# First loads into the third stage buffer, more loads ahead of the first store, and two loads issued as unequal pieces

## The chip, the cores and the metric

The kernel runs on one core of a Trainium2 chip (trn2); the other cores are idle. The metric is device time in microseconds, median of the fast runs. A profile is one execution; its span leaves out some 2 us of the time. PE is the matrix engine, DVE the vector engine, ACT the scalar engine and SP the engine that issues most transfers; HBM is the large memory, SBUF the memory beside the engines, PSUM the small one that PE writes. Transfers run on sixteen DMA engines; "the queue" is what has been issued and has not landed.

## The reference, cut to what matters

```python
batch, seq, heads, dim = 16, 512, 16, 64            # all float32
q1, q2 = q[..., :32], q[..., 32:]
q_rot = concat([q1 * cos - q2 * sin, q1 * sin + q2 * cos])   # k_rot likewise
scores = einsum('bshd,bthd->bsht', q_rot, k_rot)    # 16 x 512 x 16 x 512
```

Inputs are 67 MB, the output is 268 MB. Every byte crosses between HBM and SBUF once.

## The kernel before

It has 64 stages: four for each of the 16 batches. A stage makes 4 MB of scores: DVE rotates k and q rows ("rope", three operations each), PE transposes them into a PSUM "bank", DVE or ACT copies the bank to kT_t or qT_t, PE multiplies, ACT copies scores to the stage buffer `st` (three buffers of 32 KB per partition), and SP issues the store. Loads come in pairs of row blocks, 1 MB each. Batch 0 is cut by heads instead, so that stores of 1 MB can start early. Its eight loads have runs of G x D = 256 elements, 1 KB:

```python
    def load_unit(which, u):                # batch 0: 8 loads of 512 KB
        t = in_tiles.get((which, u // 2))
        if t is None:
            t = in_tile(which, u // 2)      # takes an input buffer: k has 3, q has 2
        src = (k_v if which == "k" else q_v)[0, :, :, G * u : G * (u + 1), :]
        nc.sync.dma_start(t[:, u % 2].rearrange(...), src)
    def load_pair(which, pair):             # later batches: one load of 1 MB
        ...
        nc.sync.dma_start(t.rearrange("p c (h d) -> p c h d", h=H), src)
    ...
        for i in range(C):                  # stages 0 to 3, C = 4
            ...
            for p in range(HP):             # 8 score pairs of a stage
                scores(i, p, st)
                if p in (1, 2) and late:    # k rows of batch 1
                    bank, dst = transposed(*late.pop(0))
                    dve.pop(0)()
                    nc.vector.tensor_copy(out=dst, in_=bank)
                if p == 5:
                    ...
                    tr_act(...)             # transposes that ACT copies
                if p == 7:
                    ...
        for i in range(C, NST):             # stages 4 to 63
            ...
            if i % 2 == 1:
                load_pair("q", (i + 1) // 2 + 2)
            else:
                load_pair("k", (i + 4) // 2 + 3)
            ...
            for p in range(HP):
                scores(i, p, st)            # the store is issued with the last pair
```

## Time and profile before

| | kernel before |
|---|---|
| time | 814.07 us, median of 3 runs (811.2 to 814.53) |
| span of the profiled run | 810.0 us |
| transfers | 336.31 MB, 415 GB/s over the span, 432 by the usual time of a 32 KB packet |
| busiest compute engine | PE, 83% of the span |
| first 4 MB store issued | 79.90 us |
| last store: median of its sixteen parts, last part | 798.8, 808.9 us |

The prediction shows the lines that carry this. A store is done by sixteen DMA engines, each of which reports its own landing; the last row of the table is read from those events in the trace. Where below I give the mean idle time of the DMA engines, it is counted from the packets in the trace: the time in which an engine has no packet, averaged over sixteen.

### The profile page before, as it was taken

How to read it: one execution, taken by the hardware profiler on the slowest of the kernel's cores; microseconds unless marked ns; L12 is line 12 of the kernel's file. 1: busy time of each engine (PE TensorE's matmuls, PEld its weight loads, DVE VectorE, ACT ScalarE, POOL GpSimd, SP SyncE). 2: the span in 40 equal slices, each digit the busy share in tenths (PEclk: the TensorE clock that was granted, in tenths of full speed). 3: DMA queues.
4: the chain of work that ended last, by engine and by line, in shares of the span. 5: the costliest groups of instructions: out<-in, count | busy, mean ns of one | idle time of the engine just before them, and what ended most of it. 6: DMA issues, size and time to landing. Idle time of an engine off the chain costs nothing.

```text
span 810.0 us, 7781 instructions
## 1 busy us (share of the span) xinstructions
PE 676.1 (83%) x3072; PEld 297.1 (37%) x3072; DVE 598.7 (74%) x624; ACT 500.1 (62%) x533; POOL 0.7 (0%) x6
## 2 busy tenths in 40 slices
PE   4997999888887888978888888888888889889960
PEld 2443444333333333333333333333333334334310
DVE  7798988877777877868868688677778787786300
ACT  3884777656565675566666656665656657566770
POOL 0000000000000000000000000000000000000000
PEclk9998999999999999999999999999999999999995
DMA  8999999999999999999999999999999999999994
GB/s 272 383 424 397 426 428 426 433 418 431 434 424 432 433 422 434 433 421 438 431 420 437 432 420 438 432 420 438 432 417 442 409 421 440 428 386 435 398 417 202
DMA packets 29028, 336.31 MB, mean 415 GB/s; under 512 B 3392, under 2 KB 7744, under 8 KB 15424
## 3 DMA queue, kind: packets, MB, share of 16 engines
q1 hardware_dynamic: 27648, 335.55, 98.1%
q8 instruction: 24, 0.39, 0.2%
q10 hardware_dynamic: 1344, 0.26, 0.2%
q14 instruction: 12, 0.10, 0.0%
HBM read 67.37 MB, written 268.44 MB: 415 GB/s over the span
## 4 chain that ended last, share of the span: by engine, by line
DMA 58%; PE 22%; DVE 8%; ACT 8%; issue 1%; ACTq 0%
DMA out_dram<-st 57%; PE ps L159 16%; ACT st L166 8%; PE bank L136 6%; DVE part L118 3%; DVE k_rot L121 2%; DVE k_rot L115 1%; DVE q_rot L121 1%; DVE q_rot L115 1%; DVE qT_t L259 1%; DMA sin_k<-in_sin_dram 1%; DVE kT_t L215 0%; ACT kT_t L176 0%; ACTq L286 0%; ACTq L166 0%
## 5 line engine op out<-in xcount | busy, mean ns | idle before, releaser
L166 ACT COPY st<-ps 128x1024 f32<-128x1024 f32 x512 | 488.9, 1022 | 275.0 <-DMA out_dram<-st 176.4
L159 PE MATMUL ps<-kT_t,qT_t 64*128 64x512 f32 x2048 | 528.0, 637 | 72.1 <-ACT st L166 69.4
L159 PEld LDWEIGHTS ps<-kT_t,qT_t 64*128 64x128 f32 x2048 | 183.6, 194 | 255.3 <-issue 148.3
L259 DVE COPY qT_t<-bank 128x512 f32<-128x512 f32 x118 | 81.6, 691 | 135.7 <-PE bank L136 135.1
L136 PE MATMUL bank<-ident,k_rot 128*128 128x128 f32 x512 | 84.6, 291 | 35.7 <-DVE k_rot L121 35.6
L136 PEld LDWEIGHTS bank<-ident,k_rot 128*128 128x128 f32 x512 | 55.1, 143 | 132.7 <-DVE k_rot L121 69.0
L136 PEld LDWEIGHTS bank<-ident,q_rot 128*128 128x128 f32 x512 | 58.4, 149 | 99.8 <-issue 74.8
L259 DVE COPY kT_t<-bank 128x512 f32<-128x512 f32 x112 | 77.0, 688 | 24.2 <-PE bank L136 24.2
L136 PE MATMUL bank<-ident,q_rot 128*128 128x128 f32 x512 | 90.0, 304 | 1.9 <-DVE q_rot L121 1.9
L121 DVE TENSOR_TENSOR k_rot<-k_rot,part 128x1024 f32<-128x1024 f32 x64 | 78.4, 1224 | 2.1
L115 DVE TENSOR_TENSOR q_rot<-q_sb,cos_q 128x1024 f32<-128x1024 f32 x64 | 78.0, 1219 | 0.0
L121 DVE TENSOR_TENSOR q_rot<-q_rot,part 128x1024 f32<-128x1024 f32 x64 | 77.8, 1216 | 0.2
L118 DVE TENSOR_TENSOR part<-q_sb,ss_q 128x1024 f32<-128x1024 f32 x64 | 77.8, 1216 | 0.0
L115 DVE TENSOR_TENSOR k_rot<-k_sb,cos_k 128x1024 f32<-128x1024 f32 x64 | 77.8, 1216 | 0.0
L118 DVE TENSOR_TENSOR part<-k_sb,ss_k 128x1024 f32<-128x1024 f32 x64 | 77.8, 1216 | 0.0
L176 ACT COPY kT_t<-bank 128x512 f32<-128x512 f32 x10 | 5.6, 619 | 6.6 <-PE bank L136 6.6
L215 DVE COPY kT_t<-bank 128x512 f32<-128x512 f32 x6 | 4.1, 685 | 4.5 <-PE bank L136 4.5
L176 ACT COPY qT_t<-bank 128x512 f32<-128x512 f32 x10 | 5.6, 618 | 2.6 <-PE bank L136 2.6
L59 DVE COPY ss_k<-sin_k 128x128 f32<-128x128 f32 x1 | 0.2, 227 | 5.3 <-DMA sin_k<-in_sin_dram 5.3
L176 ACT ACT_TABLE_LOAD x1 | 1.3, 1283 | 2.9 <-issue 2.9
masks.py:199 POOL TENSOR_SCALAR_AFFINE_SELECT ident<-ident 128x128 f32<-128x128 f32 x1 | 0.3, 292 | 0.1
L60 DVE TENSOR_SCALAR ss_q<-sin_q 128x128 f32<-128x128 f32 x1 | 0.2, 222 | 0.0
(7 smaller groups left out, 1.0 us busy)
## 6 DMA issues: line engine op xcount, KB each, us to landing
out_dram<-st SPq DMA_DIRECT2D x60, 4096.0 KB, 28.1
k_sb<-in_k_dram SPq DMA_DIRECT2D x30, 1024.0 KB, 19.1
q_sb<-in_q_dram SPq DMA_DIRECT2D x30, 1024.0 KB, 27.2
out_dram<-st SPq DMA_DIRECT2D x16, 1024.0 KB, 9.9
k_sb<-in_k_dram SPq DMA_DIRECT2D x4, 512.0 KB, 7.0
q_sb<-in_q_dram SPq DMA_DIRECT2D x4, 512.0 KB, 8.4
cos_k<-in_cos_dram ACTq DMA_DIRECT2D x1, 64.0 KB, 4.2
sin_k<-in_sin_dram ACTq DMA_DIRECT2D x1, 64.0 KB, 4.1
```

The costliest lines, as they stand in the source:

```text
L59: nc.vector.tensor_copy(out=ss[:, :, 0, :], in_=tabs["sin", which])
L60: nc.vector.tensor_scalar_mul(ss[:, :, 1, :], tabs["sin", which], -1.0)
L115: lambda: nc.vector.tensor_tensor(a.rearrange(v1, **k1), src.rearrange(v1, **k1), cs, op=mult),
L118: lambda: nc.vector.tensor_tensor(bt.rearrange(v1, **k2), src.rearrange(v1, **k2), ss, op=mult),
L121: lambda: nc.vector.tensor_tensor(a4, a4, swapped, op=add),
L136: nc.tensor.transpose(bank[:, x, :], src, ident)
L159: nc.tensor.matmul(out=ps[:, r, :], lhsT=lhs[64 * r : 64 * r + 64, :], rhs=rhs[64 * r : 64 * r + 64, :], start=True, stop=True,)
L166: nc.scalar.copy(out=st[:, 2 * p : 2 * p + 2, :], in_=ps)
L176: nc.scalar.copy(out=dst, in_=bank)
L215: nc.vector.tensor_copy(out=dst, in_=bank)
L259: nc.vector.tensor_copy(out=dst, in_=bank)
```

## The change

It has four parts. Batch 0 goes into the third stage buffer, in four loads, of which the larger two have 3 KB runs. That leaves the input buffers free, so that seven megabytes instead of five are asked for before the first store and two more loads come between the first stores. In stages 0 to 3 the transposes move to earlier score pairs and the tables are built on ACT; after that the load of a stage moves behind its store. Last, k pairs 16 and 20 are issued as nine pieces of unequal size.

```diff
-        nc.vector.tensor_copy(out=ss[:, :, 0, :], in_=tabs["sin", which])
-        nc.vector.tensor_scalar_mul(ss[:, :, 1, :], tabs["sin", which], -1.0)
+        nc.scalar.copy(out=ss[:, :, 0, :], in_=tabs["sin", which])
+        nc.scalar.mul(ss[:, :, 1, :], tabs["sin", which], -1.0)
...
+    PIECES = {
+        ("k", 16): (15, 14, 12, 10, 8, 7, 4, 10, 48),
+        ("k", 20): (15, 13, 11, 9, 6, 5, 3, 2, 64),
+    }
...
+    st_first = [stage_pool.tile([P, H, S], fp32, tag="stage", name="st") for _ in range(2)]
+    early = stage_pool.tile([P, 2 * C * H * D], fp32, tag="stage", name="early")
...
-        nc.sync.dma_start(t.rearrange("p c (h d) -> p c h d", h=H), src)
+        t = t.rearrange("p c (h d) -> p c h d", h=H)
+        p0 = 0
+        for n in PIECES.get((which, pair), (P,)):
+            nc.sync.dma_start(t[p0 : p0 + n], src[p0 : p0 + n])
+            p0 += n
...
-        for u in range(2):
-            load_unit("k", u)
-            load_unit("q", u)
-        for which in ("k", "q"):
-            for u in range(2, C):
-                load_unit(which, u)
+        for head, heads in ((0, G), (G, H - G)):
+            load_units("k", head, heads)
+            load_units("q", head, heads)
         load_pair("k", 2)
+        load_pair("q", 2)
+        load_pair("k", 3)
...
-                if p in (1, 2) and late:
+                if p in (0, 1) and late:
...
+                if i == 0 and p == 1:
+                    load_pair("k", 4)
+                if i == 0 and p == 3:
+                    load_pair("q", 3)
+                if p in (2, 6):
...
-            if i % 2 == 1:                      # stages 4 to 63: ahead of the score pairs
-                load_pair("q", (i + 1) // 2 + 2)
-            else:
-                load_pair("k", (i + 4) // 2 + 3)
...
+            if i % 2 == 1:                      # now behind the store
+                load_pair("q", (i + 1) // 2 + 2)
+            else:
+                load_pair("k", (i + 4) // 2 + 3)
```

More of the change, by code (lines that the diff above doesn't have):

```diff
@@ L71, in in_tile, with load_units @@
         return t
-    def load_unit(which, u):
-        t = in_tiles.get((which, u // 2))
-        if t is None:
-            t = in_tile(which, u // 2)
-        src = (k_v if which == "k" else q_v)[0, :, :, G * u : G * (u + 1), :]
-        nc.sync.dma_start(t[:, u % 2].rearrange("p (c h d) -> p c h d", c=C, h=G), src)
+    st_first = [stage_pool.tile([P, H, S], fp32, tag="stage", name="st") for _ in range(2)]
+    early = stage_pool.tile([P, 2 * C * H * D], fp32, tag="stage", name="early")
+    units = {}
+    def load_units(which, head, heads):
+        n = C * heads * D
+        t = early[:, load_units.used : load_units.used + n]
+        load_units.used += n
+        t = t.rearrange("p (c e) -> p c e", c=C)
+        src = (k_v if which == "k" else q_v)[0, :, :, head : head + heads, :]
+        nc.sync.dma_start(t.rearrange("p c (h d) -> p c h d", d=D), src)
+        for h in range(0, heads, G):
+            units[which, (head + h) // G] = t[:, :, D * h : D * (h + G)]
+    load_units.used = 0
     def load_pair(which, pair):
@@ L87, in load_pair @@
         src = (k_v if which == "k" else q_v)[b, :, 2 * x : 2 * x + 2]
-        nc.sync.dma_start(t.rearrange("p c (h d) -> p c h d", h=H), src)
+        t = t.rearrange("p c (h d) -> p c h d", h=H)
[3 more added lines that the diff above has]
+            p0 += n
     rots = {}
     def rope(which, n):
-        src = in_tiles[which, n // 2][:, n % 2]
         a = rot_pool.tile([P, H * D], fp32, tag="rot_" + which, name=which + "_rot")
@@ L99, in rope @@
         if n < C:
+            src = units[which, n]
+            sv = "p c (g j) -> p c g j"
             v1 = "p (c g j) -> p c g j"
@@ L105, in rope @@
         else:
+            src = in_tiles[which, n // 2][:, n % 2]
+            sv = "p (g j) -> p g j"
             v1 = "p (g j) -> p g j"
@@ L115, in rope @@
             lambda: nc.vector.tensor_tensor(
-                a.rearrange(v1, **k1), src.rearrange(v1, **k1), cs, op=mult
+                a.rearrange(v1, **k1), src.rearrange(sv, j=HD), cs, op=mult
             ),
             lambda: nc.vector.tensor_tensor(
-                bt.rearrange(v1, **k2), src.rearrange(v1, **k2), ss, op=mult
+                bt.rearrange(v1, **k2), src.rearrange(sv, j=D), ss, op=mult
             ),
@@ L184 @@
         load_tables("q", "(p c) j -> p c j")
-        for u in range(2):
-            load_unit("k", u)
-            load_unit("q", u)
-        for which in ("k", "q"):
-            for u in range(2, C):
-                load_unit(which, u)
+        for head, heads in ((0, G), (G, H - G)):
+            load_units("k", head, heads)
+            load_units("q", head, heads)
         load_pair("k", 2)
+        load_pair("q", 2)
+        load_pair("k", 3)
         make_identity(nc, ident)
         build_table("k")
+        build_table("q")
         run(rope("k", 0))
         tr_act("k", 0)
-        build_table("q")
         run(rope("q", 0))
@@ L201 @@
         for i in range(C):
-            st = stage_pool.tile([P, H, S], fp32, tag="stage", name="st")
+            st = st_first[i] if i < 2 else stage_pool.tile([P, H, S], fp32, tag="stage", name="st")
             late = []
@@ L207 @@
                 dve = rope("k", i + 1) + rope("q", i + 1) + rope("k", C + i)
+                nxt = [("k", i + 1), ("q", i + 1)]
             else:
                 dve = rope("q", C) + rope("k", C + i) + rope("q", C + 1) + rope("k", 2 * C)
+                nxt = [("q", C), ("k", C + i)]
             for p in range(HP):
                 scores(i, p, st)
-                if p in (1, 2) and late:
+                if p in (0, 1) and late:
                     bank, dst = transposed(*late.pop(0))
@@ L215 @@
                     nc.vector.tensor_copy(out=dst, in_=bank)
-                if p == 5:
-                    run(dve[: 3 if i == 0 else 1])
-                    dve = dve[3 if i == 0 else 1 :]
-                    tr_act(*(("k", i + 1) if i < C - 1 else ("q", C)))
-                if p == 7:
-                    run(dve[:3])
-                    dve = dve[3:]
-                    tr_act(*(("q", i + 1) if i < C - 1 else ("k", C + i)))
-            run(dve)
-            if i == 0:
-                load_pair("k", 3)
-                load_pair("q", 2)
-            elif i == 2:
-                load_pair("k", 4)
-                load_pair("q", 3)
+                if i == 0 and p == 1:
[3 more added lines that the diff above has]
+                if p in (2, 6):
+                    m = len(dve) - (6 if p == 2 else 3) + (-3 if i == C - 1 else 0)
+                    run(dve[:m])
+                    dve = dve[m:]
+                    tr_act(*nxt.pop(0))
+            run(dve)
+            if i == 1:
                 load_pair("k", 5)
```

## The prediction

> **What bounds the kernel now.** I read the page of the kernel before from the top: busy shares, slices, then the groups of instructions, then the chain that ended last, and last the table of windows for the first 80 us and the last 30 us.
>
> ```profile
> PE 676.1 (83%) x3072; PEld 297.1 (37%) x3072; DVE 598.7 (74%) x624; ACT 500.1 (62%) x533; POOL 0.7 (0%) x6
> DMA  8999999999999999999999999999999999999994
> GB/s 272 383 424 397 426 428 426 433 418 431 434 424 432 433 422 434 433 421 438 431 420 437 432 420 438 432 420 438 432 417 442 409 421 440 428 386 435 398 417 202
> DMA packets 29028, 336.31 MB, mean 415 GB/s; under 512 B 3392, under 2 KB 7744, under 8 KB 15424
> ...
> out_dram<-st SPq DMA_DIRECT2D x60, 4096.0 KB, 28.1
> ```
>
> No compute engine is full; the transfers are: tenths of 9 in every slice but the first and last, about 430 GB/s in the middle. A slice is 20.25 us. 336.31 MB at 430 GB/s would take 782 us, so of the span of 810.0 us some 28 us are lost, and the low numbers say where: 272, 383 and 397 in the first four slices, 386 and 398 near the end, 202 in the last. A 4 MB store lands 28.1 us after its issue though it moves in 9.7 us, so the queue is normally some 18 us deep: short waits of the compute engines cost nothing in the middle. In the chain of waits 57% is stores landing; before 140 us it is instead a run of DVE and PE pieces.
>
> The windows of the start (columns: stretch, length, busy time and count of PE, PEld, DVE, ACT, POOL, then granted clock, DMA share, GB/s):
>
> ```profile
> 6.00:8.00 2.00, 0.00 (x0) 0.00 (x0) 1.97 (x3) 0.00 (x0) 0.00 (x0) 1.00 1.10 357
> 16.00:18.00 2.00, 2.00 (x8) 0.93 (x6) 2.00 (x3) 0.84 (x1) 0.00 (x0) 1.00 0.93 369
> 18.00:20.00 2.00, 2.00 (x10) 0.86 (x10) 1.97 (x3) 1.62 (x3) 0.00 (x0) 1.00 0.03 10
> 20.00:22.00 2.00, 2.00 (x11) 0.70 (x8) 2.00 (x3) 2.00 (x3) 0.00 (x0) 1.00 0.79 328
> ```
>
> While the first batch comes in 1 KB runs the rate is about 350. At 18 us the five megabytes asked for are in and the first store is issued only at 19.59 us: the transfers stand still for about 2.5 us. The same view at the end:
>
> ```profile
> 796.00:798.00 2.00, 0.00 (x0) 0.00 (x0) 0.00 (x0) 0.00 (x0) 0.00 (x0) 0.50 1.18 508
> 798.00:800.00 2.00, 0.00 (x0) 0.00 (x0) 0.00 (x0) 0.00 (x0) 0.00 (x0) 0.50 0.16 66
> 802.00:804.00 2.00, 0.00 (x0) 0.00 (x0) 0.00 (x0) 0.00 (x0) 0.00 (x0) 0.50 0.11 49
> ```
>
> From 798 us on only one to three of sixteen engines still move bytes. The trace's sixteen landing times of the last store say it exactly: thirteen parts at 798.8 to 798.9 us, the others at 800.7, 804.4 and 808.9. The slowest DMA engine alone makes the end, 10.1 us after the bulk. In the same landing times its lag grows from nothing at 84 us to 13 us at 714 us, one engine in steps of about 0.27 us per stage. So two things can shorten this kernel: bytes that move earlier in the first 80 us, and less work or less idling for that one engine.
>
> **What the Trainium skill says.** (1) "DMA: Bandwidth & Descriptors", Where 436 GB/s comes from: sixteen ports give 435 GB/s. The trace agrees: a 32 KB packet takes 1213 ns, which for 16 engines is 432 GB/s. (2) Same page, Why small descriptors are slow: a fixed cost per packet. The trace agrees: 1 KB packets took 48 ns at the median, 4 KB 159, 8 KB 309. (3) Same page, Why a DMA increments its semaphore by 16: a transfer uses the largest k up to 16 that divides the slow dimension, the lowest-numbered engines. No run of before shows a k under 16; the last part of the change rests on it. (4) Same page, Latency and other measured facts: engines 7 and 15 are usually slower. The trace shows two slow engines but not their numbers.
>
> **The change part by part.**
>
> *3 KB runs.* Of the 4 MB of batch 0, 1 MB keeps 1 KB runs, 3 MB get 3 KB runs. From the packet times (about 8 ns + 37 ns per KB, estimated from the four sizes) a 3 KB packet should take 120 ns against 3 x 48 = 144. Per engine 64 of these: 64 x 24 ns = 1.5 us gained.
>
> *Loads ahead of the first store.* The early data lie in the third stage buffer, so the input buffers are free and 7 MB instead of 5 MB are asked for before the first store, two more loads following between the stores of the first stage. 2 MB are 4.9 us of transfers, more than the pause of 2.5 us; the pause goes. Together about 4 us, perhaps 5 with the slow packets around 30 us (254 GB/s in one window), by 40 us.
>
> *But what takes the place of the pause.* The loads and the 16 MB of batch 0 are 27 MB up to the first 4 MB store. In before they were just drained at 79.3 us and that store is issued at 79.90, after one load: the pause there is 0.5 us. In after they drain 4 to 5 us earlier, near 75 us, and the next load now comes behind that store, so the transfers stand until the store is issued. Its time is set by DVE, which in the chain is the run from 29.9 to 66.7 us (about 1.14 us per operation, no gap). What the change does to DVE: the four table operations go to ACT and the ropes no longer wait for them, about 0.6 us (first rope 5.61 to about 5.0). In the timeline before, DVE stood from 24.74 to 29.20 us for a transpose of the k rows of batch 1 that sits behind the second score pair of stage 1. That now follows the first pair, and the transposes of stage 0 come at its third and seventh pair instead of sixth and eighth; I estimate the copy near 26 us. So the DVE run shifts by about 3.2 us, the first 4 MB store to about 76.7 us. With the 0.9 us that the first store took from issue to first packet (19.59 to 20.5), transfers resume at 77.6, against about 79.9 before. **The start is worth 2.3 us**, not 5; the rest of the 5 waits at that store.
>
> *The unequal pieces.* k pair 16 goes as 15, 14, 12, 10, 8, 7, 4, 10, 48 partitions, k pair 20 as 15, 13, 11, 9, 6, 5, 3, 2, 64. By the rule for k, the highest engine gets 3 + 4 = 7 partitions instead of 16, the lowest 11 + 12 = 23, in a slope between. A partition is two packets of 4 KB, 0.32 us: the highest engine loses 9 x 0.32 = 2.9 us of work, the lowest gain 7 x 0.32 = 2.2 us. If the slow engine is the highest, the end comes 2.9 us sooner; if it is a low one, up to 2.2 us later. Against it stands a wait that I see in the built program's order: completion semaphores are used in rotation, eight of them, and each transfer waits for the one eight before. With nine pieces the fourth already waits for a store two stages back, the eighth for the store just ahead of it, the ninth for the first piece. So SP holds the next store back until that store has landed on its slowest engine. The fast engines run dry, for about the lag of 5 us at that time; that costs nothing, for they have 10 us in hand at the end. The highest engine has no partition of pieces 1 to 7, so it stands from its end of the store to the start of piece nine, 0.9 us plus two issues of 0.35 us: 1.6 us, twice 3.2 us. Low engines have 2.2 us of pieces to cover it. Sum for the slow engine: highest, -2.9 + 3.2 = +0.3; lowest, +2.2; in the middle about 0. **I put the pieces at +0.5 us** before allowing for what the author may have seen.
>
> *Later loads moved behind the stage's store.* The q load goes some 7 us later and lands about one load, 2.4 us, after its own stage's store. Its rope runs three stages on, when that store's buffer is free. DVE has 12.1 us per stage in steady state and needs 10.1 (6 x 1.22 + 4 x 0.69), so it bears this. About 0.
>
> Sum: 814.07 - 2.3 + 0.5 = 812.3. I take 811.0, because a change with sizes so particular is likely to have been chosen after a measured gain from the slow engine.
>
> **The rivals.** (a) The whole early gain is kept: if stage 4's store is issued near 75 us, 5 us come through, and if the slow engine is the highest with little idling, 2.9 more: 806. For it: DVE's pause in stage 0 is 4.46 us and could vanish. Against: the 12 operations of stage 3. (b) The third buffer is missed: stage 2 reuses the first stage buffer and its first eviction near 36 us must wait for stage 0's four stores, 13 MB into the queue, about 35.5 us. A wait of a few us there would eat the gain: 814. For it: the two times are that close. Against: PE and DVE can go on for three score pairs. (c) The pieces stop the queue for longer than I think, so that the slow engine stands too: 4 to 6 us lost, 816. (d) Clearing the lag helps the end: with fast engines re-aligned twice, the lag of 10.1 us at the end falls to 5 or so. For it: the landings show alignment after every dry spell. Against: the slow engine's own bytes and stalls stay, and it ends the span; the fast ones then only end later.
>
> **Range and chances.** Start 0.5 to 5 us of gain, pieces between 4 us of gain and 4 us of loss; runs of before lie between 811.2 and 814.53. That gives 804 to 816. A gain of 2% would be 16.3 us, more than the tail and the start's pause together, a loss of 2% has no cause here: 3% and 1%.
>
> **What would show each step.** 3 KB packets at 120 ns and no window near zero at 18 us; the DVE pause after 24.7 us shortened to about 2 us; the first 4 MB store near 76.7 us and a pause of transfers of 2 to 4 us before it; around stages 22 and 30 a spell of low GB/s and landing times drawn together, SP waiting on a transfer; at the end a lag of the last engine of 5 to 8 us. It is wrong if the first 4 MB store is issued much sooner, or if the slowest engine's own work between 80 us and the end is not the same within 3 us.

## The result, and the profile after

The changed kernel takes 814.44 us (814.28 to 815.51, four runs), the kernel before 813.71 in the same rounds. The ratio is 1.0017, with an interval of 0.9993 to 1.0041: no difference. A ratio here is the mean time of one kernel's fast runs over the mean of the other's of the same rounds, so it is not quite the ratio of the medians.

So a change in four parts cancels itself out. The slices of the changed kernel say where to look. First line: DMA busy share in tenths; second: GB/s, per slice of 20.3 us.

```profile
DMA  9997999999999998999999999999999999999995
GB/s 343 423 424 332 390 436 419 432 436 425 429 430 430 431 431 315 427 418 441 426 332 418 433 435 425 427 431 435 420 435 432 421 438 427 435 431 426 436 436 247
```

The first slices have what was wanted: 343 and 423 instead of 272 and 383. But the fourth slice has fallen from 397 to 332, and two new holes stand in the middle, 315 and 332, where the kernel before had 434 and 420. The fourth slice and the first of the two new holes in windows of 2 us each (stretch, length, busy time and count of PE, PEld, DVE, ACT, POOL, granted clock, DMA share, GB/s):

```profile
74.00:76.00 2.00, 2.00 (x12) 1.11 (x12) 1.40 (x3) 1.42 (x3) 0.00 (x0) 1.00 0.12 47
76.00:78.00 2.00, 1.60 (x9) 0.39 (x5) 1.97 (x3) 2.00 (x3) 0.00 (x0) 1.00 0.00 0
...
312.00:314.00 2.00, 0.42 (x2) 0.00 (x0) 1.97 (x3) 0.68 (x1) 0.00 (x0) 1.00 0.27 59
314.00:316.00 2.00, 1.92 (x10) 1.11 (x12) 2.00 (x4) 1.18 (x2) 0.00 (x0) 1.00 0.31 76
316.00:318.00 2.00, 2.00 (x12) 0.72 (x8) 1.61 (x3) 1.76 (x2) 0.00 (x0) 1.00 1.26 293
318.00:320.00 2.00, 2.00 (x12) 1.11 (x12) 2.00 (x3) 1.03 (x2) 0.00 (x0) 1.00 0.92 336
```

At 74 us the transfers have nothing left to do and stand for 4.7 us. At 312 us they stand again; and from 316 to 320 us, although the DMA share is about 1, only 293 and 336 GB/s move. That last pair of windows turned out to be the important one.

The timeline of SP shows the cause of the hole at 312 us (start, length, line, what is issued):

```profile
289.50 0.34 SPq L192 DMA_DIRECT2D out_dram<-st  x1
289.94 25.29 SPq L105 DMA_DIRECT2D k_sb<-in_k_dram  x9
315.32 0.38 SPq L192 DMA_DIRECT2D out_dram<-st  x1
```

The nine pieces occupy SP for 25.29 us, and the next store, whose last scores ACT had copied by 299.96 us, goes out only at 315.32 us. Below, such a hold of SP with the hole that follows is called a stop. SP's waits say what it waited for (engine, line, what, then total, times, longest):

```profile
SPq L105 <- DMA out_dram<-st: 37.0, 4, 9.7
```

Four waits of a load for a store's landing, 37 us in all, in a kernel that had none before. The order of the built program explains it: completion semaphores go round in eight, so the eighth piece waits for the store just ahead of the pieces and the ninth for the first piece.

One more group is new. DVE waits for the q loads, which now come behind the store:

```profile
L136 DVE TENSOR_TENSOR q_rot<-q_sb,cos_q 128x1024 f32<-128x1024 f32 x60 | 73.2, 1221 | 118.9 <-DMA q_sb<-in_q_dram 118.9
```

The last number is idle time of DVE, 118.9 us, put down to the q loads. It is a large item. Whether it costs anything is a question for an experiment (e3).

### The profile page after: what moved, and what is told of

The parts are those of the page before. It is cut to its first block, busy times and chain, and to the rows that moved or that the text cites. A ratio compares the mean times of both kernels' runs of the same rounds, so it can differ in the third digit from the quotient of the medians.

```text
span 812.5 us, 7797 instructions
## 1 busy us (share of the span) xinstructions
PE 679.9 (84%) x3072; PEld 296.8 (37%) x3072; DVE 592.9 (73%) x620; ACT 506.8 (62%) x537; POOL 0.7 (0%) x6
## 4 chain that ended last, share of the span: by engine, by line
DMA 49%; PE 27%; DVE 16%; ACT 4%; issue 1%; SPq 1%; ACTq 0%
DMA q_sb<-in_q_dram 42%; PE ps L180 19%; PE bank L157 8%; DVE part L139 4%; ACT st L187 4%; DMA k_sb<-in_k_dram 3%; DVE k_rot L142 3%; DMA out_dram<-st 3%; DVE q_rot L136 2%; DVE qT_t L273 2%; DVE kT_t L273 1%; DVE q_rot L142 1%; DVE k_rot L136 1%; SPq L192 1%; DMA sin_k<-in_sin_dram 1%
## 5 line engine op out<-in xcount | busy, mean ns | idle before, releaser
L187 ACT COPY st<-ps 128x1024 f32<-128x1024 f32 x512 | 494.4, 1018 | 271.8 <-PE ps L180 187.8
L180 PE MATMUL ps<-kT_t,qT_t 64*128 64x512 f32 x2048 | 533.9, 643 | 15.8 <-ACT st L187 15.7
L136 DVE TENSOR_TENSOR q_rot<-q_sb,cos_q 128x1024 f32<-128x1024 f32 x60 | 73.2, 1221 | 118.9 <-DMA q_sb<-in_q_dram 118.9
L273 DVE COPY kT_t<-bank 128x512 f32<-128x512 f32 x112 | 76.7, 685 | 13.7 <-PE bank L157 13.7
L139 DVE TENSOR_TENSOR part<-k_sb,ss_k 128x1024 f32<-128x1024 f32 x60 | 72.9, 1215 | 0.0
L139 DVE TENSOR_TENSOR part<-q_sb,ss_q 128x1024 f32<-128x1024 f32 x60 | 72.8, 1214 | 0.0
L136 DVE TENSOR_TENSOR k_rot<-k_sb,cos_k 128x1024 f32<-128x1024 f32 x60 | 72.8, 1214 | 0.0
L136 DVE TENSOR_TENSOR k_rot<-early,cos_k 128x1024 f32<-128x1024 f32 x4 | 4.9, 1220 | 5.0 <-DMA cos_k<-in_cos_dram 5.0
L139 DVE TENSOR_TENSOR part<-early,ss_k 128x1024 f32<-128x1024 f32 x4 | 4.9, 1218 | 0.2 <-ACT ss_k L60 0.2
L136 DVE TENSOR_TENSOR q_rot<-early,cos_q 128x1024 f32<-128x1024 f32 x4 | 4.9, 1217 | 0.0
L139 DVE TENSOR_TENSOR part<-early,ss_q 128x1024 f32<-128x1024 f32 x4 | 4.9, 1217 | 0.0
```

What stands on the lines that cost most here:

```text
L136: lambda: nc.vector.tensor_tensor(a.rearrange(v1, **k1), src.rearrange(sv, j=HD), cs, op=mult),
L139: lambda: nc.vector.tensor_tensor(bt.rearrange(v1, **k2), src.rearrange(sv, j=D), ss, op=mult),
L180: nc.tensor.matmul(out=ps[:, r, :], lhsT=lhs[64 * r : 64 * r + 64, :], rhs=rhs[64 * r : 64 * r + 64, :], start=True, stop=True,)
L187: nc.scalar.copy(out=st[:, 2 * p : 2 * p + 2, :], in_=ps)
```

## The experiments

My theory after reading the two traces: the start gains a little, as predicted; the pieces lose it again. The rivals: the two stops of the transfers are free, because the fast DMA engines have 10 us in hand at the end; the stops are paid in full; the late q loads cost; the unequal shares cost or pay.

### e1: the pieces taken out

```diff
-    PIECES = {("k", 16): (15, ...), ("k", 20): (15, ...)}
+    PIECES = {}
```

> The changed kernel with both loads whole again, nothing else. In the changed kernel's trace the transfers of most engines stand for 3.4 us at 310 to 316 us and 2.5 us at 414 to 418 us while SP holds the next store behind the ninth piece, and the last engine then ends 7.2 us after the median one instead of 10.1. Theory (the slowest engine sets the end; a stop that makes all wait for it turns a maximum of sums into a sum of maxima): half comes back, about 811.5 us, bulk of the last store landing near 799, last part 10 us later. Rival 1 (the stops are paid in full): 808.6. Rival 2 (the stops are free, because only engines with time in hand stood): 814.4, same as the changed kernel.

Measured: 809.7 us, ratio to before 0.9968 (0.9953 to 0.9984). The last store's median part lands at 796.1 us and its last part at 805.6. So the rest of the change gains 0.3%, 2.6 us, and the pieces cost the difference of the ratios, 1.0017 - 0.9968 = 0.0049 or 4.0 us. From the two intervals the uncertainty of that is some 2.3 us, so the pieces are not free, but whether they cost half or the whole 5.8 us for which the sixteen engines stood on average (rival 1) these two kernels can't tell; e5 and e6 can. At 312 us the profile without the pieces has no hole:

```profile
312.00:314.00 2.00, 0.46 (x4) 0.42 (x4) 1.97 (x3) 0.14 (x1) 0.00 (x0) 1.00 1.18 502
316.00:318.00 2.00, 2.00 (x13) 1.03 (x12) 1.62 (x3) 1.42 (x3) 0.00 (x0) 1.00 1.02 442
```

### e2: the pieces alone, in the kernel before

```diff
+    PIECES = {("k", 16): (15, 14, 12, 10, 8, 7, 4, 10, 48),
+              ("k", 20): (15, 13, 11, 9, 6, 5, 3, 2, 64)}
-        nc.sync.dma_start(t.rearrange("p c (h d) -> p c h d", h=H), src)
+        (the loop over the pieces, as in the change)
```

> The kernel before with the two unequal loads alone. Theory: slower by 2 to 3 us than before (816), with two stops of the transfers and the end's lag down to about 7 us. Rival 1 (paid in full): plus 5.8 us, 819.5. Rival 2 (free): within 0.5 us of before, 813.7; a gain of 2.9 us if the slow engine were the highest one.

Measured: 819.59 us, ratio 1.0101 (1.0073 to 1.0129). That is 8.2 us slower than before in the same rounds (interval 5.9 to 10.5), so the theory of 2 to 3 us was wrong; rival 1, paid in full, lies at the edge of the interval. The DMA engines stand for 7.9 us on average in the two stops, against 5.8 in the changed kernel: here the load is issued ahead of its stage's store, so that the queue probably holds less when it is cut off. I did not separate how much of the larger loss comes from that.

### e3: the loads back ahead of the score pairs

```diff
 (from e1; stages 4 to 63)
+            if i % 2 == 1:
+                load_pair("q", (i + 1) // 2 + 2)
+            else:
+                load_pair("k", (i + 4) // 2 + 3)
             st = stage_pool.tile(...)
             for p in range(HP):
                 ...
-            (the same four lines behind the loop)
```

> As e1_nopieces, but from the second batch on the load of a stage is issued ahead of its score pairs, as in the kernel before. In the changed kernel DVE waited 119 us in all for q loads that come behind the store. Theory (the queue is 18 us deep, so DVE's wait is hidden): the same time as e1 within 1 us, DVE's wait for q loads gone and ACT's wait for stores back near 170 us. Rival (the late q loads thin out the queue and cost the end): 2 us or more faster than e1.

Measured: 809.0 us, ratio 0.9962 (0.9947 to 0.9977), the same as e1. The wait of DVE for q loads is gone from the groups, and the idle time has moved back to where it was in the kernel before:

```profile
L184 ACT COPY st<-ps 128x1024 f32<-128x1024 f32 x512 | 489.3, 1022 | 271.3 <-DMA out_dram<-st 167.9 <-PE ps L177 94.1 <-PE bank L154 5.0
```

ACT stands 167.9 us for stores to land. In steady state the compute engines are faster than the transfers and must stand somewhere: with one order DVE stands for its loads, with the other ACT stands for its buffers. The 118.9 us were no cost.

### e4: six copies moved from DVE to ACT

```diff
 (from e1; the k rows of batch 1, stages 1 to 3)
                     dve.pop(0)()
-                    nc.vector.tensor_copy(out=dst, in_=bank)
+                    nc.scalar.copy(out=dst, in_=bank)
```

> As e1_nopieces, but the six copies of transposed k rows in stages 1 to 3 are made by ACT instead of DVE. Theory (DVE's run sets the first 4 MB store, and the transfers stand for 4.7 us before it): DVE saves 6 x 0.69 = 4.1 us, so that store is issued near 74.5 us instead of 77.9 and the time is 3 us below e1. Rival (PE or ACT sets that store): the store within 1 us of 77.9 and the time as e1.

Measured: 805.42 us, ratio 0.9913 (0.9898 to 0.9929), faster than e1 by 0.0055 or 4.5 us. The first 4 MB store goes out 4.0 us earlier, and the transfers hardly stand ahead of it, 0.36 us (SP's timeline of e1, then of this kernel; then its window of 2 us):

```profile
77.30 0.34 SPq L189 DMA_DIRECT2D out_dram<-st  x1
```

```profile
73.25 0.34 SPq L189 DMA_DIRECT2D out_dram<-st  x1
```

```profile
72.00:74.00 2.00, 1.60 (x12) 0.60 (x8) 1.97 (x3) 2.00 (x3) 0.00 (x0) 1.00 0.85 344
```

Mean idle time of the DMA engines up to 100 us: 6.7 us in e1, 2.85 here. So the pause at 74 us is where most of the early gain went, and DVE's run of ropes and copies is what set it.

### e5 and e6: the stop without the unequal shares, twice and four times

```diff
 (from e1)
+    PIECES = {("k", n): (16,) * 8 for n in (16, 20)}            # e5
+    PIECES = {("k", n): (16,) * 8 for n in (12, 16, 20, 24)}    # e6
```

> The changed kernel, but the two loads as eight equal pieces of 16 partitions each: every engine has one partition of every piece, so no engine gets more or less than in e1_nopieces, while the eighth piece and the next store still wait in SP for the store ahead. Theory (what costs is the stop and the restart, not the unequal shares): the two stops are there again in the transfers, and the time lies 2 to 5 us above e1_nopieces (0.9968 of before), so 0.999 to 1.003 of before. Rival (the unequal shares cost, the slow engine got 10 partitions where it had 8): the same as e1_nopieces within 1 us, 0.9965 to 0.998.

> As e5_equal2 with four loads in eight equal pieces (k pairs 12, 16, 20, 24), so twice the stops. Theory: twice the loss of e5_equal2 against e1_nopieces, 4 to 10 us, 1.002 to 1.009 of before. Rival (a stop only re-aligns engines, which happens once): about the loss of e5_equal2 again.

Measured: e5 814.68 us, ratio 1.0035 (1.0023 to 1.0048); e6 820.43 us, ratio 1.0105 (1.0089 to 1.012). Against e1 that is 5.4 us for two stops and 11.1 us for four, some 2.7 us for each, with the same share of every load for every engine. (e1 ran in other rounds on another chip; against e7 below, which has no stop and ran in the same rounds, it is 5.2 and 10.9 us.) The unequal shares are not needed for the loss, and the rival for e6, that re-aligning the engines happens only once, falls; both times are a little above what I had allowed for. SP's waits for stores double with the stops (e5, then e6):

```profile
SPq L102 <- DMA out_dram<-st: 36.7, 4, 9.8
```

```profile
SPq L102 <- DMA out_dram<-st: 74.5, 8, 9.8
```

The standing does not measure the loss either: between 150 and 550 us the DMA engines stand for 3.1 us on average in e5 and for 3.0 us in e6, with twice the stops and twice the loss. That rules out rival 1 of e1. The landings show where the time goes. This is how much later than in e1 the last part of a 4 MB store lands, in the profiled runs:

```
us later than e1     ahead of the stops   after each stop          last store
the changed kernel          0.6           2.7, 6.0                     6.1
e5, equal pieces            0.5           2.6, 6.3                     8.6
e6, equal pieces            0.6           3.5, 5.6, 8.2, 11.2         11.3
```

The last DMA engine falls behind by 2 to 4 us at each stop and keeps that to the end; only e5 loses 2.3 us more later, without a stop. (The profiled runs differ more than the medians: that of e1 is the fastest of its six, that of e5 the slowest.)

Why is a stop not free, when the last DMA engine still has pieces to move in it? The packets tell a part. Usually a packet of 4 KB takes 159 ns, one of 8 KB 309 and one of 32 KB 1213. I summed what the packets between 150 and 550 us took above that, per engine:

```
kernel                  stops   above the usual, us per engine
the kernel before         0          1.5
e1, no pieces             0          1.2
e4                        0          1.0
e10, e4 once more         0          4.9
e2, pieces alone          2          5.9
the changed kernel        2          6.0
e5, equal pieces          2          7.3
e6, equal pieces          4         14.7
```

That is 2.2 to 3.4 us per stop, close to the 2.7 us of the measured times. Slow packets occur without stops too: e10 has 4.9 us of them, but spread out, at most 1.0 us in any 20 us (e3, e7 and e9 have 1.4, 2.3 and 3.1). In the changed kernel the 4 KB packets that start between 316 and 320 us take 330 ns on average, up to 1.09 us, and the 32 KB packets 1444 ns; in e1 the 32 KB packets of the same stretch take 1215. This is the pair of windows with full DMA share and low GB/s. All engines start again together, and for some microseconds packets are slow; by the landings above the last engine loses time too.

A common start alone does not do it, though. At 78 us, after the pause, all sixteen engines of the changed kernel start together with a store, and its 112 packets of 32 KB take 1229 ns on average, 1271 at most. Slow packets come at 87 us, where the engines, still in step, pass to the next load: 2024 ns for the sixteen 32 KB packets that start between 87 and 88 us, then 246 ns for the 4 KB packets up to 92 us. e4 hardly stands ahead of that store and has the same spell (1741 ns at 82 to 84 us, then 220). And at the stop the 4 KB packets of the pieces are slow already at 310 to 314 us, before the restart (249 ns). So all engines meeting a load in step is a rival to the restart as the cause; no run here separates the two, or shows why such packets are slow.

### e7: the highest engine relieved, without a stop

```diff
 (from e1)
+    PIECES = {("k", n): (120, 8) for n in (16, 20)}
```

> The changed kernel, but the two loads as 120 and 8 partitions: engines 0 to 14 take 8 of the first piece, engines 0 to 7 one of the second, the highest engine nothing, and two pieces are too few to hold SP. So the highest engine has 16 partitions, 5 us, less to do. Theory (the slow engine is one of numbers 4 to 6, as the landings of the pieces tell): as e1_nopieces, or 0.6 us slower, 0.997 to 0.998 of before. Rival (the slow engine is the highest): up to 5 us below e1_nopieces, 0.991 of before.

Measured: 809.74 us, ratio 0.9971 (0.9958 to 0.9984), the same as e1. Taking 5 us of work from the highest-numbered engine gains nothing: it is not the one that ends last. SP's waits of this kernel have none for a store's landing but the one at the end, so two pieces make no stop.

The landings of the changed kernel's pieces say more. The store ahead of k pair 16 has its last part at 314.56 us, when the median part is at 310.4. The same late engine is seen in the piece of 15 partitions (last part 314.86), in those of 14, 12, 10, 8 (316.38) and 7 (316.80), but not in that of 4 (last part 313.59). A piece of n partitions runs on the n lowest engines by the rule that the prediction cites. The trace agrees with it on how many: the piece of 15 has fifteen landings, and one more event at its issue, which the rule's page also states. Which ones, no view shows; the numbers rest on the page. By it the slow engine is one of numbers 4 to 6 at this point of the run. The pieces gave those engines 8 to 10 partitions of each load instead of 8, in both loads together 18 to 20 instead of 16: 0.6 to 1.3 us more work, not less.

### e8: the copies on ACT in the kernel before

```diff
 (from the kernel before)
-                    nc.vector.tensor_copy(out=dst, in_=bank)
+                    nc.scalar.copy(out=dst, in_=bank)
```

> The kernel before with the six copies of transposed k rows in stages 1 to 3 made by ACT instead of DVE, as in e4_lateact. In the kernel before the transfers stood for only 0.5 us ahead of the first 4 MB store, so DVE's run hardly bound there. Theory (early transfers and DVE's run only pay together): within 1 us of before, 0.999 to 1.001. Rival (the copies on ACT pay by themselves, as 4 us in e4_lateact): 0.995 of before.

Measured: 811.69 us, ratio 0.9993 (0.998 to 1.0005): nothing clear of noise. The first 4 MB store goes out earlier here too, at 76.37 us instead of 79.90:

```profile
76.37 0.36 SPq L171 DMA_DIRECT2D out_dram<-st  x1
```

But there the queue is still full at that time. The change without its pieces gains 2.6 us (e1), the faster DVE run alone nothing clear of noise (e8), both together 7 us (e4: 0.0087 of 812.7; once more, in e10, 6 us).

### e9 and e10: work moved to engines 0 to 3

```diff
 (from e4)
+    PIECES = {("k", n): (112, 4, 4, 4, 4) for n in range(8, 24, 2)}
```

> As e4_lateact, and eight k loads (pairs 8, 10 to 22) as 112 partitions and four times 4: engines 0 to 3 take 7 + 4 partitions, all others 7 instead of 8, and five pieces do not hold SP until the store has landed. So engines 4 to 15 have 8 partitions, 2.5 us, less to do in the whole run and engines 0 to 3 24 partitions, 7.6 us, more. Theory (one engine of 4 to 15, most likely 4 to 6, makes the end, 10 us after the bulk, and engines 0 to 3 have that time in hand): 1.5 to 2.5 us faster than e4_lateact in the same rounds, the last part of the last store some 3 us nearer the bulk. Rival (the end belongs to the sum of the bytes, or one of 0 to 3 is slow too): the same or up to 5 us slower.

> The kernel of e4_lateact once more, as the measure for e9_low4 on the same chip and in the same rounds: 0.991 of before, with the first 4 MB store issued near 73 us.

Measured in the same rounds: e9 803.59 us, ratio 0.9894 (0.9866 to 0.9921); e10, which is e4 once more, 807.66 us, ratio 0.9925 (0.9896 to 0.9953). The intervals overlap, so a gain of e9 over e10 is not established. The expected mechanism is not confirmed either: in e9 the last part of the last store still lands 9.5 us behind the median one, no nearer the bulk. In its k load of pair 22 (issued at 337.4 us) the pieces of 4 partitions contain the last landing (365.76 us), so after most of the extra work one of engines 0 to 3 is last. What I can say is that forty pieces that do not hold SP cost nothing that can be seen, and that both e4 and e9 beat the kernel before and the changed kernel.

## Why the prediction was right or wrong

The measured 814.44 us lies in the range of 804 to 816 and within 2%, as forecast. The central 811.0 is 3.4 us low. The range is 12 us wide, wider than any single term, so the hit alone says little of the mechanism. Its steps one by one:

- **3 KB runs: right.** Packets of 3 KB took 121 ns at the median; 120 was estimated.
- **The pause at 18 us goes: right.** The first store is issued at 19.29 us with the queue still full; up to 60 us the DMA engines stand for 2.2 us on average, against 4.9 before.
- **A pause ahead of the first 4 MB store takes its place: right, and larger.** It was predicted at 2 to 4 us with the store at 76.7 us; it is 4.7 us, and the store is at 77.88. Most of that is the copy in stage 1, estimated near 26 us and seen at 27.66: DVE stood for 3.54 us instead of 2 (the line below, changed kernel). e4 shows by intervention that this run of DVE sets the store.

```profile
27.66 0.69 DVE L237 COPY kT_t<-bank 128x512 f32<-128x512 f32 x1 [3.54 <-PE bank L157]
```

- **The start is worth 2.3 us: right in sum.** e1, the change without the pieces, gains 2.6 us (interval 1.3 to 3.8). By 100 us only part of it is there: the bytes moved by then put e1 1.2 us ahead of before. The rest is spread over the remaining run, and I did not trace it.
- **Later loads about 0: right.** e3 differs from e1 by 0.0006.
- **The unequal pieces, +0.5 us: the step that was mis-sized.** e1 and the changed kernel differ by 4.0 us. The stop itself was foreseen with its cause, the semaphores in rotation, down to the piece that waits. The sentence that failed is "The fast engines run dry, for about the lag of 5 us at that time; that costs nothing". The loss does not go with the standing, but a stop is not free: the last DMA engine loses 2 to 4 us at each, with 2.2 to 3.4 us of slow packets per engine, which the prediction's sum for the slow engine had no term for. e5 and e6 show that the loss goes with the number of stops.
- **Its own sign of being wrong came.** It asked for the slowest engine's work from 80 us to the end to be the same within 3 us. Taken as the time from the last part of the first 4 MB store to that of the last store, it is 714.5 us before, 721.6 in the changed kernel and 716.1 in e1.
- **The allowance of 1.3 us towards the author's intent: wrong.** The prediction took 811.0 instead of its own sum of 812.3 because sizes so particular would rest on a measured gain from the slow engine. e1 and e2 show only a loss, and e7 that the highest engine is not the slow one.
- **Rivals.** Rival (c), pieces that stop the queue for longer, comes nearest, but it blamed standing of the slow engine. Rival (d), re-aligning helps the end: the last part does land nearer the median one, 7.2 us behind instead of 10.1, but the median part comes 5.6 us later, as (d) itself allowed. Rival (a) needed the first 4 MB store near 75 us; it came at 77.88, and e4, where it comes at 73.25 us, takes 805.42 us, near the 806 of (a). Rival (b) did not come: up to 60 us no wait of ACT for a store's landing is listed.

What stays open: why packets are slow around a stop, why e2 lost 4 us per stop and e5 2.7, and which engine ends the span, since the late one is not always the same.

## What to carry to other kernels

Bytes moved earlier pay only as far as something is ready to be stored when they are through: look for the first point at which the queue runs dry after the change, and ask which engine sets it. Before cutting a transfer into pieces, count the completion semaphores: a burst as long as their rotation (eight here) makes the issuing engine wait for its own first piece and lets a deep queue run empty. Idle time of an engine that is faster than the bound can move from wait to wait without any cost, here 118.9 us of it.

## What the Trainium skill lacked or had wrong

- "DMA: Bandwidth & Descriptors", Latency and other measured facts, names engines 7 and 15 as usually slower. Its best guess at a cause is specific to transfers issued by GpSimd; those here are issued from SP, so the runs do not contradict the page. For them it lacks which engine is late: in the changed kernel at 314 us one of 4 to 6 (4.2 us behind the median), in e9 at 365 us one of 0 to 3, and 5 us less work for engine 15 changed nothing (0.9971 against 0.9968).
- No page has what it costs when the queues of all sixteen engines run dry and they start again together: 4 KB packets of 330 ns instead of 159 between 316 and 320 us, 2.2 to 3.4 us per engine and stop in sum, and 2.7 us of time per stop in e5 and e6.
